# One PSUM bank for four state space transposes, and one adaLN section read in half rows in a later stage

## The chip, the cores and the metric

The kernel runs on one core of a Trainium2 chip. The metric is the device time of one execution in microseconds (us), lower is better. The core has five engines with instruction streams of their own: TensorE (PE, matmuls and transposes into PSUM), VectorE (DVE), ScalarE (ACT), GpSimd (POOL) and SyncE (SP, which here issues nearly all DMAs). Each takes its own instructions in order; between engines only semaphores order them.

## The reference, cut to what matters

One decoder layer in float32, sequence 2048, width 1024. Half of the mixing width is attention with forget gates (8 heads of 64), the other half a complex diagonal state space model (32 groups of 16 channels, 64 states each). A conditioning vector `c` makes six vectors of width 1024 (adaLN): shift, scale and gate for the mixer, and the same for the FFN.

```python
silu_c = jax.nn.silu(c)
mod = (silu_c @ w_ada[l] + b_ada[l])[:, None, :]
sh_m, sc_m, gt_m, sh_f, sc_f, gt_f = jnp.split(mod, N_MOD, axis=-1)

h = rmsnorm(x, g_mix[l]) * (1.0 + sc_m) + sh_m
q, k, v, f_logit, u = jnp.split(h @ w_in[l], [...], axis=-1)
attn = rmsnorm(forgetting_attention(q, k, v, log_f), g_attn_out[l])
ssm = rmsnorm(s5_ssm(u, ...), g_ssm_out[l])
x = x + gt_m * (jnp.concatenate([attn, ssm], axis=-1) @ w_out[l])

h = rmsnorm(x, g_ffn[l]) * (1.0 + sc_f) + sh_f
gate_pre, val = jnp.split(h @ w_up[l], 2, axis=-1)
y = (jax.nn.silu(causal_dwconv(gate_pre, ...)) * val) @ w_down[l]
x = x + gt_f * y
```

In the state space part the output is gated: `z = gelu(y)`, then `z * sigmoid(z @ w_glu + b_glu)`, per group.

## The kernel before

The sequence is cut into four blocks of 512 tokens. A float32 matmul is made of three: each operand is split into a high and a low part (`w_hi`, `w_lo`, `h_hi`, `h_lo`), and hi x hi, hi x lo and lo x hi are accumulated in PSUM. Results that a later stage needs go through DRAM scratch (`qb_d`, `kb_d`, `v_d`, `u_d`, `att_d`, `ssm_d`, `f_d`).

**What sets the order.** The program is written stage by stage. A planner then orders each engine's stream: it walks a model of the timeline, and where several instructions could go next on an engine, it takes the one that stands earliest in the program; what is written under `tc.high_priority()` goes first. The order is fixed when the kernel is built. On the chip each engine follows its stream, so an instruction whose data are late holds all that follow it on that engine. Tiles of one tag form a ring of `bufs` buffers, given out in program order: a tile waits until the last reader of the one before it in that buffer is done. When a pool is closed, the next pool takes its place in memory and waits for its last users, for single tiles where the pool was opened through `opened`.

**The input stage** (to about 350 us in the profile). The u projections of blocks 2, 3, 1 and 0 (`proj_u`), the q, k and v projections of blocks 1 and 0 (`proj_qkv`), the tables of the state space part, the forget gates' running sums, and the adaLN sections. Sections 0 and 1 are made first (`ada_first`). The other four go through `ada_late`: `ada_acc` reads the section in 8 row blocks of 128 x 1024 (512 KB, L305), in tiles of the ring `xt` with six buffers, and accumulates them with DVE (L307 the first, L309 the other seven) into `ada_acc`, a ring of two. `ada_cols` then sums over the partitions with 8 matmuls against a column of ones (L315) and adds the bias (L317), which gives the vector as 8 columns, one per 128 channels. Section 5 is `tf`, the FFN's gate; section 2 is `tm`, the mixer's gate. Both are loaded behind the forget gates, `tf` first, and their columns are made by the hook of `proj_qkv(0, ...)` behind its sixth q/k unit, when `tf` and `tm` both are pending. Then `in_ctx.close()` frees the pools of this stage, which hold the x tiles, the adaLN tiles and most PSUM banks.

**The state space stage** (to about 620 us). `ssm` goes over 16 pairs of channel groups; `stage_a` of pair p + 1 is written ahead of `stage_b` of pair p. It runs at high priority. `stage_a` loads the pair's tables (`tab`, `ft`, `ttg`, `glt`), transposes the inputs, makes the state inputs (L834) and runs the scan on DVE. `stage_b` makes the outputs (`y_ps`, L860 to L862), GELU on ACT and DVE (`z`, L869, a ring of two), the gate matmuls (`g_ps`, L874), tanh on ACT (`th`, L877), the product on DVE (L880, which writes over `th`), and the transposes back to tokens (`tr_ps`, L885), copied out by ACT (`vout`, L886). `g_ps` and `tr_ps` share the tag `out`, a ring of one PSUM bank. After every fourth pair `vout` goes to `ssm_d`.

Beside it, in program order: attention of block 0 (`attention((0,))`), then the q, k and v projections of blocks 2 and 3, which read their normalised inputs back from `f_d`. Each `proj_qkv` has 8 units for q and k (`qk`, L460) and 8 for v (L427). Their PSUM banks are `vq` and `qs`; attention's scores use the tag `sc`, a ring of two banks (`max_ps`, `am_ps`).

**Attention of one head.** `att_max` loads q into `qa` and each key block into one of the `ka` tiles, finds the row maxima (L938, L943), transposes them into a row `rrow` (L949, L951), and SP copies that into `qa` (L952). `att_main` makes the scores (L981, L982), the exponentials (L991 to L993) and the sums over values (L1002, L1006). Finished pairs of heads go to `att_d` (L1039). There are five `ka` tiles in the attention pool; a sixth, `kx`, joins for blocks 1 to 3.

**After it.** `mix_t(0)` reads attention and state space outputs back (L1178, L1179), norms the state space half (squares L1181, scale L1187), transposes it (L1191, into the ring `ff` of three banks that takes the place of projection and state space banks), splits it, and norms the attention half (L1198). Then come `out_proj(0)` (L1217), attention of blocks 1 to 3, and the FFN. `tf` is read where the down projection is added to the residual (L1279, L1419).

Of the kernel before, what the change touches and what calls it, by code (L numbers as in the profile page):

```python
# [12 lines left out]
F32 = mybir.dt.float32  # L13
F32R = mybir.dt.float32r
# [27 lines left out]
RT = 1  # L42
ATB = 1
HOOK = 5
LEAD = 4
NSC = 2

# [63 lines left out]
def hybrid_layer(ctx, tc, x, c_t, w_ada, b_col, gains, w_flat, bf_row, a_re, a_im, log_dt,  # L111
# [336 lines left out]
                Q.dma_start(u_d[t0 : t0 + P, (cc - 2) * 256 : (cc - 1) * 256], ust)  # L448
        return h

    def proj_qkv(b, h, vq_ps, hook=None):
        def qk(ms):
            ws = [weights.get(*qk_slots[m]) for m in ms]
            pss = [vq_ps() for _ in ms]
            for k in range(KT):
                hi, lo = h[k]
                for (wh, wl), ps in zip(ws, pss):
                    a, bb = wh[:, k * P : (k + 1) * P], wl[:, k * P : (k + 1) * P]
                    for i, (lt, rt) in enumerate(((a, hi), (a, lo), (bb, hi))):
                        mark[0] = T.matmul(ps, lhsT=lt, rhs=rt, start=(k == 0 and i == 0), stop=(k == KT - 1 and i == 2))  # L460
            for m, ps in zip(ms, pss):
                hi = vq_a("qk_hi", [P, TB], F32R)
                lo = vq_b("qk_lo", [P, TB], F32R)
                sc = 0.125 if m < 4 else 1.0
                A.activation(hi, ps, AF.Copy, scale=sc)
                V.scalar_tensor_tensor(out=lo, in0=ps, scalar=sc, in1=hi.bitcast(F32), op0=ALU.mult,
                                       op1=ALU.subtract)
                dst = qb_d[b] if m < 4 else kb_d[b]
                for g in range(2):
                    hd, rs = (m % 4) * 2 + g, slice(g * 64, (g + 1) * 64)  # L470
                    Q.dma_start(dst[hd, int(m < 4)], hi[rs].bitcast(F32))
                    Q.dma_start(dst[hd, int(m >= 4)], lo[rs].bitcast(F32))

        for ms in ((0,), (1,), (2,), (3,), (4,), (5,), (6,), (7,)):
            qk(ms)
            if ms == (HOOK,) and hook is not None:
                hook()
        for cc in range(2):
            sl = [weights.get(*vfu_slots[cc * 2 + kh][:2]) for kh in range(2)]
            for s in range(4):  # L480
                ps = vq_ps()
                token_rows([ps], h, s, sl, 256)
                pv = ps[:, 0:256].rearrange("p (h d) -> p h d", d=64)
# [3 lines left out]
                Q.dma_start(v_d[b][s, :, cc * 4 : cc * 4 + 4], vst.bitcast(F32))  # L487
# [310 lines left out]
    def ssm(sp, sps):  # L798
# [56 lines left out]
        def stage_b(p, vout, ft, ttg, glt, ug, hs):  # L855

            yp = sps.tile([P, 512], F32, name="y_ps", tag="y", bufs=1)
            for g in range(2):
                yo = yp[:, g * 256 : (g + 1) * 256]
                T.matmul(yo, lhsT=ttg[:, g, :], rhs=ug[:, g, :], start=True, stop=False)  # L860
                T.matmul(yo, lhsT=ft[:, 0, g], rhs=hs[:, 0, 0:256], start=False, stop=False)
                T.matmul(yo, lhsT=ft[:, 1, g], rhs=hs[:, 1, 0:256], start=False, stop=True)  # L862

            y2 = sp.tile([P, 512], F32, name="y2", tag="y2", bufs=1)
            A.activation(y2, yp, AF.Square, scale=math.sqrt(0.044715))
            V.scalar_tensor_tensor(out=y2, in0=y2, scalar=1.0, in1=yp, op0=ALU.add, op1=ALU.mult)
            A.activation(y2, y2, AF.Tanh, scale=math.sqrt(2.0 / math.pi))
            z = sp.tile([P, 512], F32, name="z", tag="z")
            V.scalar_tensor_tensor(out=z, in0=y2, scalar=1.0, in1=yp, op0=ALU.add, op1=ALU.mult)  # L869

            gp = sps.tile([P, 512], F32, name="g_ps", tag="out", bufs=1)
            th = sp.tile([P, 512], F32, name="th", tag="th")
            for g in range(2):
                T.matmul(gp[:, g * 256 : (g + 1) * 256], lhsT=glt[:, g, :], rhs=z[:, g * 256 : (g + 1) * 256],  # L874
                         start=True, stop=True)
# [4 lines left out]
            V.scalar_tensor_tensor(out=o4, in0=th, scalar=1.0, in1=z, op0=ALU.add, op1=ALU.mult)  # L880
            c0 = (p % 4) * 32
            for kb in range(2):
                pt = sps.tile([P, 512], F32, name="tr_ps", tag="out", bufs=1)
                for g in range(2):
                    T.transpose(pt[:, g * P : (g + 1) * P], o4[:, g * 256 + kb * P : g * 256 + (kb + 1) * P], ident)  # L885
                A.activation(vout[kb][:, :, c0 : c0 + 32].rearrange("k t (g c) -> k g t c", g=2),  # L886
                             pt[:, 0:256].rearrange("k (g t c) -> k g t c", g=2, t=8), AF.Copy, scale=0.25)

        vin = vout = None
        pend = None  # L890
# [185 lines left out]
    def ada_late(sec, key):  # L1076
        late_acc.append((ada_acc(sec, V), sec, key))

    def ada_cols():

        with tc.issue_after(mark[0].ins):
            while late_acc:
                acc, sec, key = late_acc.pop(0)
                ada_col(acc, prep_ps, sec, mod[key])

    ap_ = in_ctx.enter_context(tc.tile_pool(name="ada", bufs=1))
    with tc.tile_pool(name="prep", bufs=1) as pp, tc.tile_pool(name="wu", bufs=1) as wup:
        rows0 = load_x(2)
# [14 lines left out]
        forget()  # L1103
        ada_cols()
        fold_gain(mod["gf"], 8)
        ada_late(5, "tf")
        ada_late(2, "tm")
    proj_qkv(0, h, pair_ps(qs_psum), ada_cols)
    in_ctx.close()
    att_ctx = ExitStack()  # L1110
    att_pool = opened(att_ctx, "att", bufs=2, side="right")
    def aug_tiles(pool, nm, n):

        ts = [pool.tile([67, TB], F32R, name=f"{nm}{i}", bufs=1) for i in range(n)]
        for t in ts:
            G.memset(t[64:67, :].bitcast(F32), 1.0)
        return ts

    qa_t, ka_all = itertools.cycle(aug_tiles(att_pool, "qa", 2)), aug_tiles(att_pool, "ka", 5)
    ka_t = [itertools.cycle(ka_all)]  # L1120
    att_ps = opened(att_ctx, "att_ps", bufs=1, space=PSUM, side="right")
    with tc.tile_pool(name="ssm", bufs=2) as sp, tc.tile_pool(name="ssm_ps", bufs=1, space=PSUM) as sps:
        qs_ps = pair_ps(sps)
        with tc.high_priority():
            ssm(sp, sps)
        attention((0,))
        for b in (2, 3):
            h = []
            for k in range(KT):
                f = h_f()  # L1130
                Q.dma_start(f, f_d[b][k])
                h.append(split_h(f, mod["sm"][:, k : k + 1]))
            proj_qkv(b, h, qs_ps)


    cv = const.tile([P, NFF, 4], F32, name="cv")
# [9 lines left out]
    actp = opened(fp_ctx, "act", bufs=6)  # L1146
    sq_pool.append(fp)
    yt = []
    ka_t.append(itertools.cycle(ka_all + aug_tiles(fp, "kx", 1)))

    def ff_ps():
        return fps.tile([P, 512], F32, name="ff_ps", tag="ff", bufs=3)
# [538 lines left out]
```

## Time and profile before

| | us |
|---|---|
| median of 3 runs | 2689.65 |
| lowest and highest of them | 2687.12 to 2692.45 |
| the profiled execution's own time | 2689.94 |
| its span, first to last instruction | 2687.6 |
| PE busy in the span | 2576.9 (96%) |
| PE weight loads | 2081.5 (77%) |
| DVE busy | 1928.3 (72%) |
| ACT busy | 1239.2 (46%) |
| POOL busy | 190.5 (7%) |

How to read it: the profile is one execution, and its times count from the first instruction. In a timeline a row gives the start, the length, the engine, the line, the operation with output and inputs, and in brackets how long the engine had been idle and what released it. In a group of instructions (all that touch a tile, or a line) stand the count, the least, median and most ns of one, and the first and last start in us. A table of stretches gives for each its length, then busy us and instruction count of PE, PEld (weight loads), DVE, ACT and POOL, the mean granted PE clock, the busy share of the DMA engines and GB/s. A matmul's length is modelled and overlaps the next one's, so a full PE shows as busy for the whole stretch.

### The profile page before, as it was taken

What the parts mean: (1) busy time and instruction counts of PE and PEld (TensorE: products, weight loads), DVE (VectorE), ACT (ScalarE), POOL (GpSimd) and SP (SyncE); (2) the same over time, 40 slices, a digit from 0 to 9 for tenths busy, and PEclk for the clock granted to TensorE, in tenths of its full rate; (3) what the DMA queues carried; (4) which work ended last, traced back from release to release, by engine and by line L of the source; (5) the groups of instructions that cost most, each with busy time, mean ns of one, the idle gap of its engine ahead of it and who ended that gap; (6) DMA issues with size and microseconds to landing.
All of it is one profiled execution on the core that took longest, in us unless ns stands there. A gap on an engine that the chain in (4) does not pass through costs nothing. (4 is left out here: it accounts for less than half of the span.)

```text
span 2687.6 us, 35574 instructions
## 1 busy us (share of the span) xinstructions
PE 2576.9 (96%) x12343; PEld 2081.5 (77%) x12343; DVE 1928.3 (72%) x3559; ACT 1239.2 (46%) x2056; POOL 190.5 (7%) x146
## 2 busy tenths in 40 slices
PE   6999989998999999999999999999979999999997
PEld 3888768886777888888788888887858888877886
DVE  7989678876687877887976776655587777762333
ACT  3423245554365545555555555555444444442222
POOL 0001000000000000000000000000043343310000
PEclk8999989997899999999899999999989999999999
DMA  9486977665556555656465555557622323336563
GB/s 314 146 278 214 314 239 206 200 190 163 183 186 208 195 188 176 196 171 210 165 198 193 196 174 188 174 180 279 207 102 94 126 94 105 115 124 244 199 223 96
DMA packets 263043, 500.61 MB, mean 186 GB/s; under 512 B 26800, under 2 KB 111664, under 8 KB 262864
## 3 DMA queue, kind: packets, MB, share of 16 engines
q1 hardware_dynamic: 261040, 493.10, 56.0%
q0 software_dynamic: 1280, 4.20, 0.4%
q8 instruction: 97, 1.59, 0.2%
q10 hardware_dynamic: 544, 1.05, 0.1%
q14 instruction: 82, 0.67, 0.1%
HBM read 371.17 MB, written 127.01 MB: 185 GB/s over the span
## 5 line engine op out<-in xcount | busy, mean ns | idle before, releaser
L77 DVE TENSOR_TENSOR w_lo<-w_raw,w_hi 128x1024 fp32r<-128x1024 f32 (+2 forms) x219 | 236.0, 1079 | 206.3 <-ACT w_hi L76 202.2
L76 ACT CAST w_hi<-w_raw 128x1024 fp32r<-128x1024 f32 (+2 forms) x219 | 203.3, 929 | 367.8 <-PE acc_ps L1460 112.7
L1243 PE MATMUL ff_ps<-h_hi,w_lo 128*128 128x512 f32 x704 | 280.3, 398 | 0.0
L1243 PE MATMUL ff_ps<-h_hi,w_hi 128*128 128x512 f32 x704 | 280.0, 399 | 0.1
L1243 PE MATMUL ff_ps<-h_lo,w_hi 128*128 128x512 f32 x704 | 279.6, 397 | 0.0
L943 DVE TENSOR_REDUCE mx<-sc_ps 128x1 f32<-128x512 f32 (+2 forms) x320 | 195.4, 620 | 86.7 <-PE sc_ps L938 47.9
L991 ACT ACTIVATE pf<-sc_ps 128x512 f32<-128x512 f32 (+1 forms) x320 | 168.8, 542 | 186.7 <-PE sc_ps L982 87.1
L992 ACT CAST ph<-pf 128x512 fp32r<-128x512 f32 (+1 forms) x320 | 177.6, 568 | 86.5 <-PE o_ps L1002 83.4
L993 DVE TENSOR_TENSOR pl<-pf,ph 128x512 fp32r<-128x512 f32 (+1 forms) x320 | 195.1, 620 | 22.3 <-ACT ph L992 20.9
L1001 DVE TENSOR_TENSOR acc<-acc,pf 128x512 f32<-128x512 f32 (+2 forms) x264 | 159.4, 606 | 29.6 <-ACT pf L991 27.0
L1243 PEld LDWEIGHTS ff_ps<-h_hi,w_hi 128*128 128x128 f32 x704 | 133.5, 190 | 29.1 <-ACT h_hi L378 0.5
L1243 PEld LDWEIGHTS ff_ps<-h_lo,w_hi 128*128 128x128 f32 x704 | 133.5, 190 | 29.0
L1243 PEld LDWEIGHTS ff_ps<-h_hi,w_lo 128*128 128x128 f32 x704 | 133.3, 189 | 28.8
L1459 PE MATMUL acc_ps<-act,w_hi 128*128 128x512 f32 (+1 forms) x372 | 144.5, 389 | 10.6 <-DMA act<-act 6.4
L106 ACT CAST w_hi<-w_raw 128x1024 fp32r<-128x1024 f32 (+2 forms) x100 | 96.2, 962 | 123.9 <-PE ff_ps L1243 44.5
L1460 PE MATMUL acc_ps<-act,w_hi 128*128 128x512 f32 (+1 forms) x372 | 144.2, 388 | 0.0
L1461 PE MATMUL acc_ps<-act,w_lo 128*128 128x512 f32 (+1 forms) x372 | 143.7, 388 | 0.3 <-DVE w_lo L77 0.3
L1275 PE MATMUL ff_ps<-act_hi,w_hi 128*128 128x512 f32 x352 | 140.2, 399 | 0.9 <-ACT rt L366 0.9
L1276 PE MATMUL ff_ps<-act_lo,w_hi 128*128 128x512 f32 x352 | 139.4, 397 | 0.0
L1277 PE MATMUL ff_ps<-act_hi,w_lo 128*128 128x512 f32 x352 | 139.0, 396 | 0.0
L981 PE MATMUL sc_ps<-qb,kb 128*128 128x512 f32 (+2 forms) x320 | 127.9, 401 | 2.6 <-DVE mx L943 1.8
L1002 PE MATMUL o_ps<-ph,vv 128*128 128x512 f32 (+1 forms) x320 | 122.4, 383 | 1.3 <-ACT ph L992 1.3
(517 smaller groups left out, 6455.7 us busy)
## 6 DMA issues: line engine op xcount, KB each, us to landing
w_raw<-in_w_flat SPq DMA_DIRECT2D x193, 512.0 KB
w_lo<-wlo SPq DMA_DIRECT2D x68, 512.0 KB
wlo<-w_lo SPq DMA_DIRECT2D x52, 512.0 KB
w_raw<-in_w_flat SPq DMA_DIRECT2D x64, 384.0 KB
act<-act SPq DMA_DIRECT2D x44, 512.0 KB
kb<-kb SPq DMA_DIRECT2D x80, 256.0 KB
vv<-v SPq DMA_DIRECT2D x80, 256.0 KB
w_raw<-in_w_flat SPq DMA_DIRECT2D x64, 320.0 KB
```

The lines of the kernel that those rows point to most:

```text
L76: nc.scalar.copy(hi[:, :n], raw[:, :n])
L77: nc.vector.tensor_tensor(out=lo[:, :n], in0=raw[:, :n], in1=hi[:, :n].bitcast(F32), op=ALU.subtract)
L943: V.reduce_max(out=mx[:, s, ch : ch + 1], in_=ps[:, 0:n], axis=AX.X)
L991: A.activation(pf[:, cs], ps[:, cs], AF.Exp)
L992: A.copy(ph[:, cs], pf[:, cs])
L993: V.tensor_tensor(out=pl[:, cs], in0=pf[:, cs], in1=ph[:, cs].bitcast(F32), op=ALU.subtract)
L1001: eng.tensor_tensor(out=acc[j][:, cs], in0=acc[j][:, cs], in1=pf[:, cs], op=ALU.add)
L1243: T.matmul(ps, lhsT=lt, rhs=rt, start=(n == 0), stop=(n == 23))
L1275: T.matmul(ps, lhsT=a, rhs=ah[:, ts], start=(c == 0), stop=False)
L1459: T.matmul(pss[d][:, ts], lhsT=a, rhs=ah, start=st, stop=False, skip_group_check=cut)
L1460: T.matmul(pss[d][:, ts], lhsT=a, rhs=al, start=False, stop=False, skip_group_check=cut)
L1461: T.matmul(pss[d][:, ts], lhsT=bb, rhs=ah, start=False, stop=sp_, skip_group_check=cut)
```

## The change

Two edits.

1. In `stage_b`, the four transposes of a pair go into one tile of the ring `out`, all 512 columns of the bank, and the two copies by ACT follow them. Before, two transposes filled half a tile, ACT copied it, and the next two took the next tile, which is the same bank.

2. Section 5 (`tf`) leaves the input stage. A generator, `ada_mid`, makes it in two halves of 512 channels. `proj_qkv` of blocks 2 and 3 advances it by one step after each of its 8 q/k units, 16 steps in all. A step loads a half row block (128 x 512, 256 KB) and adds it with DVE; the eighth step of each half also makes 4 columns (4 matmuls and an addition) in a bank of attention's score ring. The loads use two of the five key tiles in turn (`ka3`, `ka4`), the accumulator is a ring of one in the state space pool. For that the first attention has three key tiles, and the other two are set up again (a memset each) after the projections.

```diff
-    def proj_qkv(b, h, vq_ps, hook=None):
+    def proj_qkv(b, h, vq_ps, hook=None, each=iter(())):
...
             if ms == (HOOK,) and hook is not None:
                 hook()
+            for _ in range(EACH):
+                next(each, None)
...
             c0 = (p % 4) * 32
+            pt = sps.tile([P, 512], F32, name="tr_ps", tag="out", bufs=1)
             for kb in range(2):
-                pt = sps.tile([P, 512], F32, name="tr_ps", tag="out", bufs=1)
                 for g in range(2):
-                    T.transpose(pt[:, g * P : (g + 1) * P], o4[:, g * 256 + kb * P : g * 256 + (kb + 1) * P], ident)
+                    T.transpose(pt[:, (2 * kb + g) * P : (2 * kb + g + 1) * P],
+                                o4[:, g * 256 + kb * P : g * 256 + (kb + 1) * P], ident)
+            for kb in range(2):
                 A.activation(vout[kb][:, :, c0 : c0 + 32].rearrange("k t (g c) -> k g t c", g=2),
-                             pt[:, 0:256].rearrange("k (g t c) -> k g t c", g=2, t=8), AF.Copy, scale=0.25)
+                             pt[:, kb * 256 : (kb + 1) * 256].rearrange("k (g t c) -> k g t c", g=2, t=8), AF.Copy, scale=0.25)
...
+    def ada_mid(pool, sec, key):
+
+        for hf in range(2):
+            acc = pool.tile([P, TB], F32, name="ada_mid", tag="ada_mid", bufs=1)
+            for k in range(KT):
+                wt = att_pool.tile([P, TB], F32, name="wada", tag=f"ka{3 + k % 2}", bufs=1)
+                Q.dma_start(wt, w_ada[sec, k, :, hf * TB : (hf + 1) * TB])
+                sc = sil[:, k : k + 1]
+                if k == 0:
+                    V.tensor_scalar(out=acc, in0=wt, scalar1=sc, scalar2=None, op0=ALU.mult)
+                else:
+                    V.scalar_tensor_tensor(out=acc, in0=wt, scalar=sc, in1=acc, op0=ALU.mult, op1=ALU.add)
+                if k == KT - 1:
+                    ada_col(acc, max_ps, sec, mod[key][:, hf * 4 : hf * 4 + 4], hf * 4, 4)
+                yield
...
         fold_gain(mod["gf"], 8)
-        ada_late(5, "tf")
         ada_late(2, "tm")
...
-    qa_t, ka_all = itertools.cycle(aug_tiles(att_pool, "qa", 2)), aug_tiles(att_pool, "ka", 5)
+    qa_t, ka_all = itertools.cycle(aug_tiles(att_pool, "qa", 2)), aug_tiles(att_pool, "ka", 3)
...
         attention((0,))
+        mid = itertools.chain(*(ada_mid(sp, sec, key) for sec, key in ((5, 'tf'),)))
         for b in (2, 3):
...
-            proj_qkv(b, h, qs_ps)
+            proj_qkv(b, h, qs_ps, each=mid)
...
-    ka_t.append(itertools.cycle(ka_all + aug_tiles(fp, "kx", 1)))
+    ka_t.append(itertools.cycle(ka_all + aug_tiles(att_pool, "ka", 2, 3) + aug_tiles(fp, "kx", 1)))
```

More of the change, by code (lines that the diff above doesn't have):

```diff
@@ L44 @@
 HOOK = 5
+EACH = 1
 LEAD = 4
@@ L1111, in hybrid_layer, with aug_tiles @@
     att_pool = opened(att_ctx, "att", bufs=2, side="right")
-    def aug_tiles(pool, nm, n):
-        ts = [pool.tile([67, TB], F32R, name=f"{nm}{i}", bufs=1) for i in range(n)]
+    def aug_tiles(pool, nm, n, i0=0):
+        ts = [pool.tile([67, TB], F32R, name=f"{nm}{i}", tag=f"{nm}{i}", bufs=1) for i in range(i0, i0 + n)]
         for t in ts:
```

## The prediction

> **What bounds the kernel now.** I read the page first: its span and the slices. Each digit is a fortieth of the span, 67 us.
>
> ```profile
> span 2687.6 us, 35574 instructions
> ...
> PE   6999989998999999999999999999979999999997
> ...
> PEclk8999989997899999999899999999989999999999
> ```
>
> TensorE is the bound almost everywhere, so a change pays only where PE is idle or at a lowered clock. The change touches slices 4 to 9, where two digits fall: slice 5 (PE 8) and slice 9 (PE 8, clock 7). The second view is the table of stretches; the columns used here are the length, PE busy and, after POOL's, the granted clock and the DMA share.
>
> ```profile
> 286.00:325.00 39.00, 38.89 (x243) 34.56 (x241) 29.60 (x40) 8.19 (x12) 1.00 (x2) 1.00 0.97 328
> 325.00:350.00 25.00, 14.90 (x96) 13.32 (x97) 7.49 (x17) 6.00 (x14) 0.00 (x0) 0.80 0.98 288
> 350.00:380.00 30.00, 27.91 (x144) 22.03 (x143) 27.65 (x51) 17.90 (x33) 0.00 (x0) 0.94 0.74 227
> 380.00:620.00 240.00, 238.50 (x1413) 196.65 (x1413) 191.59 (x374) 126.26 (x261) 0.52 (x1) 1.00 0.69 202
> 620.00:670.00 50.00, 38.13 (x135) 25.11 (x134) 38.24 (x96) 24.68 (x53) 0.00 (x0) 0.68 0.49 156
> ```
>
> I call length minus busy times clock the lost PE time: 25 - 14.90 x 0.80 = 13.1 us in 325 to 350, 30 - 27.91 x 0.94 = 3.8 us, 1.5 us in the long middle, and 50 - 38.13 x 0.68 = 24.1 us in 620 to 670. PE's work is the same after the change, so these 42.5 us are all that it can win here. Before 325 nothing is lost, though DMA is at 0.97.
>
> **The front, 325 to 350.** Timelines of PE, SP, DVE and POOL:
>
> ```profile
> 343.05 0.79 PE L982 MATMUL sc_ps<-qa,ka 67*128 67x512 f32 x1 [8.13 <-DMA qa<-rrow]
> ```
> ```profile
> 325.04 1.52 SPq L899 DMA_DIRECT2D vin<-u_d  x2
> ...
> 336.05 1.76 SPq L487 DMA_DIRECT2D v<-vst  x2
> 337.91 0.72 SPq L952 DMA_DIRECT2D qa<-rrow  x1
> ```
> ```profile
> L317 DVE TENSOR_TENSOR mod_tf<-prep_ps,bcol x1: 161/161/161, 306.3 to 306.3; 128x8 f32<-128x8 f32 x1
> L317 DVE TENSOR_TENSOR mod_tm<-prep_ps,bcol x1: 167/167/167, 323.9 to 323.9; 128x8 f32<-128x8 f32 x1
> ```
> ```profile
> 330.45 0.27 DVE L951 CAST rrow<-sc_ps 4x128 fp32r<-4x128 f32 x1
> ```
> ```profile
> 323.87 1.00 POOL L802 MEMSET ft<- 128x512 f32 x2 [41.40 <-PE prep_ps L315]
> ```
>
> The small row `rrow` is ready at 330.7, but SP sends it at 337.91: from 325.04 to 336.05 SP issues the first loads of the state space stage, which are ahead of it in its queue. It lands at about 343, and PE stands for 8.13 us with the rest of block 0's value projections behind it; the next matmul takes 0.79 us, twice the usual. The burst starts at 325 because the buffers of the input stage are freed then: the memset of `ft` had waited for the last column matmul of `ada_cols`, whose sum `mod_tm` follows at 323.9. The gate column `tf` was done at 306.3; `tm` comes behind it.
>
> The change takes `tf` out of this stage and leaves it `tm` alone, which then stands where `tf` stood: the buffers come free near 306 instead of 324, 18 us earlier, and the burst lies 18 us ahead of `rrow`. Eight loads of 512 KB and their DVE work go too. But the stretch 286 to 325 loses no PE time, so nothing is won in it; and the burst now meets the key stores and the value weights there, which could stall PE instead. Bounds: 0 to 13.1 us won. I take **6 us**, near the middle, since the 8.13 us have a named cause that moves, and the place that it moves to is just as full of DMA.
>
> **The transposes.** One state group pair's transposes and their evictions (count, then least, median and most ns, then first and last start); the gate matmuls of all 16 pairs; the product that comes before the gate, for the first five pairs; and DVE's timeline.
>
> ```profile
> L885 PE MATMUL tr_ps<-ident,th x4: 271/272/279, 473.3 to 478.1; 128*128 128x128 f32 x4
> L886 ACT ACTIVATE vout<-tr_ps x2: 378/382/387, 474.4 to 478.7; 128x256 f32<-128x256 f32 x2
> ```
> ```profile
> L874 PE MATMUL g_ps<-z,glt x64: 377/379/485, 387.6 to 619.1; 128*128 128x256 f32 x64
> ```
> ```profile
> L869 DVE SCALAR_TENSOR_TENSOR z<-y,y_ps x5: 670/682/687, 379.4 to 430.2; 128x512 f32<-128x512 f32 x5
> ```
> ```profile
> 483.90 0.68 DVE L880 SCALAR_TENSOR_TENSOR th<-th,z 128x512 f32<-128x512 f32 x1
> ...
> 486.87 0.66 DVE L869 SCALAR_TENSOR_TENSOR z<-y,y_ps 128x512 f32<-128x512 f32 x1
> ```
>
> The gate matmuls, both couples of transposes and the next pair's gate matmuls share one PSUM bank, so each waits for the eviction before it. From one pair's gate to the next are (619.1 - 387.6) / 15 = 15.4 us. The second couple of transposes starts some 4.7 us after the first (478.0 less 473.3; its second one is at 478.1), 3.2 us after the first eviction has ended (474.4 + 0.38), because PE is in other work by then. This cycle paces the stage, since it also holds the `z` ahead of it: `z` has two buffers, and the one at 486.87 could be written only once the product at 483.90 had read the one before the last. With four transposes at once and then two evictions, one return to PE goes, 4.7 less the 0.4 that a couple takes: 15.4 - 4.3 = 11.1 us. What is late next is the rest of the pipeline: the first five `z`, with both buffers still empty at first, came every (430.2 - 379.4) / 4 = 12.7 us. So I take 12.7 us a pair, and the stage's end comes 15 x (15.4 - 12.7) = 40 us sooner.
>
> The first eviction now waits for the second couple too, 0.4 us; no engine gets more instructions (64 transposes, 32 evictions as before). The Trainium skill's Perfetto Trace Analysis, section Matmuls, speaks against this: independent groups should rotate through banks, so that one's evacuation overlaps the next one's matmuls. Here there is no overlap to lose, with the second couple behind the eviction as it is; by the rule the cycle would be 11.5 us, which still lies under the 12.7.
>
> **What 40 us sooner is worth.** In 380 to 620 PE is full, so an earlier end of the state space stage wins nothing there: other matmuls move back. It pays after 620. SP, ACT and PE again:
>
> ```profile
> 611.43 0.32 SPq L1039 DMA_DIRECT2D att<-at  x1
> ```
> ```profile
> 623.32 0.38 ACT L886 ACTIVATE vout<-tr_ps 128x256 f32<-128x256 f32 x1 [0.53 <-PE tr_ps L885]
> ```
> ```profile
> 620.85 0.28 PE L938 MATMUL sc_ps<-ka,qa 66*128 66x256 f32 x1
> ...
> 669.10 0.78 PE L1217 MATMUL ff_ps<-yt,w_hi 128*128 128x512 f32 x1
> ```
> ```profile
> L1191 PE MATMUL ff_ps<-ident,row x16: 272/273/422, 656.8 to 660.2; 128*128 128x128 f32 x16
> ```
>
> Projections 2 and 3 end at 620.85 and the last state space eviction comes at 623.32. Its store, reload, norm, transposes and splits take until 669.10, and only block 1's attention runs beside them, badly. With the last eviction near 583, that chain lies beside dense projections. What stays exposed: the transposes use the PSUM banks that the projections held, so 669.10 - 656.8 = 12.3 us follow the projections' end, and the attention half (stored at 611.43) needs about as long. At the stretch's loss of 24.1 / 50 that is 5.9 us, so 18 us are won; bounds 0 and 24.1. I take **16 us**, because half of the moved section falls into this place.
>
> **The half rows.** The group rows of the existing sections:
>
> ```profile
> L309 DVE SCALAR_TENSOR_TENSOR ada_acc<-wada,sil,ada_acc x28: 1259/1281/1330, 142.4 to 317.8; 128x1024 f32<-128x1024 f32 x28
> ...
> L288 DVE SCALAR_TENSOR_TENSOR ada_acc<-wada,sil,ada_acc x14: 744/749/752, 16.8 to 39.4; 128x512 f32<-128x512 f32 x14
> L307 DVE TENSOR_SCALAR ada_acc<-wada,sil x4: 734/744/754, 139.3 to 298.9; 128x1024 f32<-128x1024 f32 x4
> L286 DVE TENSOR_SCALAR ada_acc<-wada,sil x2: 476/477/478, 16.3 to 27.6; 128x512 f32<-128x512 f32 x2
> ```
> ```profile
> L1279 DVE SCALAR_TENSOR_TENSOR yt<-ff_ps,mod_tf,row x16: 735/748/753, 832.1 to 1487.3; 128x512 f32<-128x512 f32 x16
> ```
>
> Removed: 0.744 + 7 x 1.281 = 9.7 us of DVE. Added: 2 x 0.477 + 14 x 0.749 = 11.4 us, where DVE is busy 191.59 of 240 us, beside PE; counted as nothing, and 11.4 us if DVE had no room. Loads are 16 of 256 KB for 8 of 512 KB, at DMA share 0.69: eight more issues on SP, about 0.3 us each like the one at 611.43, between loads of weights. The 8 column matmuls stay; two key tiles' memsets move back on an idle POOL. The result is first read at 832.1.
>
> The added wait is in the column. Its bank comes from attention's two score banks, after all of block 0's attention in program order, so the first half's column waits until about 611. The one accumulator keeps the second half from starting until then; its loads alternate two tiles. A load under pressure took 343.05 - 337.91 = 5.1 us to its reader, so a step is at most (5.1 + 0.75) / 2 = 2.9 us and eight take 23 us: the second column comes by 635. Behind it stand block 1's second score bank, two of its key tiles, and buffers that take the accumulator's place. In PE's stream the four column matmuls stand where the planner expects the bank to be free; if attention is later than that, projection and score matmuls behind them wait too, as does DVE's stream behind the second half's first row. The Trainium skill's DMA: Bandwidth & Descriptors, section Bandwidth, speaks against the halves: it wants transfers of 1 MiB or more. By the fit in its section Anatomy of one DMA (for GpSimd's path, 2.0 us plus bytes at 436 GB/s, an estimate) a half row takes 2.6 us and the eight steps 13 us, which would take the column to 625; no row here shows a lone 256 KB load.
>
> Sum: -6 - 16 = -22 us on the profiled execution's 2689.94 us (2.3 us around the span, 0.3 above the median): **2668 us**.
>
> **Rivals.**
> - Both losses go wholly: -13.1 - 24.1 = -37, 2653 us. Needs block 0's attention to end well before the projections. For it: attention gets ACT and DVE once the states are done. Against: the 12 us behind the projections.
> - Only the front pays, -6: 2684 us. The states' pace is held by the rest of the pipeline or by PE's order, and 12.7 us was measured on few pairs.
> - The lost time only moves: the burst stalls PE ahead of 325, and attention of block 0, at 611.43 as before, sets the end. 2690 us.
> - Slower: the states keep their pace, and the second half's column blocks block 1's scores. They start at 635 instead of 620.85; for 14 us the 38.13 x 0.68 / 50 = 0.52 of PE that was used goes, 7 us, and a little clock after it: +8, 2698 us. It decides once that column ends after 621 with the output projection not yet ready.
>
> **How the numbers follow.** Forecast 0.52, full 0.08, front only 0.16, moves 0.11, slower 0.13. A measurement tells about 0.2%, 5.4 us, from no change. Faster: 0.52 + 0.08 + 0.09 of the front-only case, whose 6 us lie at that bound, 0.69; same 0.07 + 0.11 = 0.18; slower 0.13. The range of 2650 to 2693 leaves out the slower case and 0.04 below. The forecast's own range is 2655 to 2680.
>
> **What would show it.** `mod_tm` near 306 and the memset of `ft` with it; no wait of 8 us for `rrow`; four transposes back to back, gates 12 to 13 us apart, the last eviction near 583; the first output projection matmul between 620 and 640; `mod_tf` in two pieces around 611 and 635. I am wrong if the gates stay 15 us apart, if block 0's attention ends later than 611, or if the clock in the 50 us before the output projection is still under 0.8.

## The result, and the profile after

| kernel | time, us (median; least to most) | profiled span, us |
|---|---|---|
| before | 2690.39 (2687.12 to 2692.45) | 2687.6 |
| changed | 2670.65 (2669.64 to 2673.3) | 2667.8 |

The ratio is 0.9934, with a 95% interval of 0.9922 to 0.9946. The forecast was 2668 us. Timed a second time, beside the experiments, the changed kernel gave 2674.2 us against 2687.6, ratio 0.9953 (0.9941 to 0.9965). So the gain is 13 to 20 us.

The same stretches as in the prediction, for the changed kernel (length, PE, PEld, DVE, ACT and POOL busy, then the granted clock, the DMA share and GB/s):

```profile
286.00:325.00 39.00, 35.85 (x202) 31.65 (x201) 19.19 (x31) 7.68 (x13) 1.00 (x2) 0.91 1.03 318
325.00:350.00 25.00, 24.67 (x178) 21.67 (x176) 19.21 (x35) 13.59 (x26) 0.00 (x0) 1.00 0.97 309
350.00:380.00 30.00, 28.12 (x140) 21.08 (x141) 28.87 (x59) 14.76 (x29) 0.00 (x0) 1.00 0.83 241
380.00:620.00 240.00, 235.90 (x1396) 197.16 (x1395) 194.32 (x376) 124.90 (x256) 1.50 (x3) 0.98 0.70 213
620.00:670.00 50.00, 44.24 (x190) 32.99 (x189) 40.19 (x93) 27.66 (x53) 0.00 (x0) 0.84 0.56 189
```

The loss in 325 to 350 has gone from 13.1 to 25 - 24.67 x 1.00 = 0.3 us, and a new one of 39 - 35.85 x 0.91 = 6.4 us has come ahead of it. The loss in 620 to 670 has fallen from 24.1 to 50 - 44.24 x 0.84 = 12.8 us, but 380 to 620 now loses 240 - 235.90 x 0.98 = 8.8 instead of 1.5: the hole behind the projections begins sooner.

The signs that the prediction listed, from the groups of instructions (count, durations in ns, first and last start) and the timelines of POOL, ACT and SP:

```profile
L318 DVE TENSOR_TENSOR mod_tm<-prep_ps,bcol x1: 161/161/161, 304.6 to 304.6; 128x8 f32<-128x8 f32 x1
```
```profile
303.84 1.00 POOL L805 MEMSET ft<- 128x512 f32 x2 [26.24 <-DMA kb<-qk_lo]
```
```profile
L877 PE MATMUL g_ps<-z,glt x64: 377/379/381, 378.4 to 563.4; 128*128 128x256 f32 x64
```
```profile
570.36 0.66 ACT L891 ACTIVATE vout<-tr_ps 128x256 f32<-128x256 f32 x2 [0.98 <-PE tr_ps L888]
```
```profile
589.74 0.32 SPq L1044 DMA_DIRECT2D att<-at  x1
```
```profile
L318 DVE TENSOR_TENSOR mod_tf<-sc_ps,bcol x2: 155/158/162, 596.0 to 617.9; 128x4 f32<-128x4 f32 x2
```
```profile
L1238 PE MATMUL ff_ps<-yt,w_hi x64: 387/393/477, 642.5 to 690.6; 128*128 128x512 f32 x64
```

The gates are (563.4 - 378.4) / 15 = 12.3 us apart (15.4 before, 12.7 forecast). The state space stage ends at 570 instead of 623, and block 0's attention at 590 instead of 611. PE's wait of 8 us for `rrow` is gone. But the first out_proj matmul comes at 642.5, just outside the 620 to 640 that the prediction gave, and the projections' last matmul ended about 612: 30.5 us between them, where the prediction had left about 12 exposed. The 50 us ahead of out_proj:

```profile
592.50:642.50 50.00, 40.13 (x223) 32.80 (x221) 33.96 (x84) 18.62 (x38) 1.50 (x3) 0.76 0.63 209
```

A clock under 0.8 there was one of the three signs by which the prediction would be wrong, and it is 0.76, so that sign came: in the tail 50 - 40.13 x 0.76 = 19.5 us are still lost.

Two places in the timelines say where the rest went. In the front, the burst of state space loads begins on SP at 305.55, and the stores of block 0's keys are now behind it. PE stops for 3.15 us at the same time. SP, PE, ACT and DVE:

```profile
305.55 1.53 SPq L904 DMA_DIRECT2D vin<-u_d  x2
...
314.90 1.27 SPq L904 DMA_DIRECT2D vin<-u_d  x2
316.27 1.43 SPq L473 DMA_DIRECT2D kb<-qk_lo  x1
```
```profile
315.76 0.58 PE L428 MATMUL vq_ps<-w_hi,h_hi 128*128 128x256 f32 x1 [3.15 <-DVE qk_lo L467]
```
```profile
311.11 0.41 ACT L827 COPY uc<-vin 128x256 f32<-128x256 f32 x1 [7.80 <-DMA vin<-u_d]
312.49 0.40 ACT L827 COPY uc<-vin 128x256 f32<-128x256 f32 x1 [0.97 <-DMA vin<-u_d]
312.80 1.04 ACT L77 CAST w_hi<-w_raw 128x1024 fp32r<-128x1024 f32 x1
313.75 0.59 ACT L466 ACTIVATE qk_hi<-vq_ps 128x512 fp32r<-128x512 f32 x1
```
```profile
313.88 1.23 DVE L78 TENSOR_TENSOR w_lo<-w_raw,w_hi 128x1024 fp32r<-128x1024 f32 x1 [7.94 <-ACT w_hi L77]
315.02 0.68 DVE L467 SCALAR_TENSOR_TENSOR qk_lo<-vq_ps,qk_hi 128x512 fp32r<-128x512 f32 x1
```

The late key store isn't what stopped PE: PE ran on at 315.76, before that store was issued (316.27). The chain goes through ACT. Two copies (`uc`) of the state space stage stand in its stream and wait for the burst's first loads, `vin`; only behind them come the cast of a weight, the eviction `qk_hi` and then DVE's `qk_lo`, which frees PE's bank.

In the tail the rows of `mix_t(0)` are loaded at 617.71, 47 us after the state space stage's last eviction and 28 us after attention's last store. Below are DVE's first and last instruction of the section's second half, PE's column matmuls, and SP:

```profile
596.06 0.48 DVE L1100 TENSOR_SCALAR ada_mid<-wada,sil 128x512 f32<-128x512 f32 x1
...
615.17 0.75 DVE L1102 SCALAR_TENSOR_TENSOR ada_mid<-wada,sil,ada_mid 128x512 f32<-128x512 f32 x1
```
```profile
615.98 1.87 PE L316 MATMUL sc_ps<-ones,ada_mid 128*128 128x1 f32 x8 [1.62 <-DVE ada_mid L1102]
```
```profile
616.70 0.47 SPq L934 DMA_DIRECT2D ka<-kb  x1
617.26 0.40 SPq L935 DMA_DIRECT2D ka<-cum  x1
617.71 0.33 SPq L1199 DMA_DIRECT2D row<-att  x1
```

The first half's column waited for block 0's attention, as forecast; the second half began when that column had freed the accumulator (596), and the row loads stand in SP's queue behind everything of it. On the chip SP waited little for the section itself from 590 to 620 (1.2 us at its loads) and longer at the stores of v (7.2 us, for the projections' results `vst`), so the rows are late by their place in SP's order rather than by a wait for the section. That the section gave them this place is a reading; the experiments test it.

### The profile page after: what moved, and what is told of

Same layout as the page of the kernel before. It is cut to its first block, busy times and chain, and to the rows that moved or that the text cites. A ratio compares the mean times of both kernels' runs of the same rounds, so it can differ in the third digit from the quotient of the medians.

```text
span 2667.8 us, 35631 instructions
## 1 busy us (share of the span) xinstructions
PE 2571.5 (96%) x12343; PEld 2082.7 (78%) x12343; DVE 1928.8 (72%) x3568; ACT 1240.3 (46%) x2056; POOL 190.4 (7%) x146
## 5 line engine op out<-in xcount | busy, mean ns | idle before, releaser
L1264 PEld LDWEIGHTS ff_ps<-h_hi,w_hi 128*128 128x128 f32 x704 | 133.1, 189 | 28.6
```

What stands on the lines that cost most here:

```text
L1264: T.matmul(ps, lhsT=lt, rhs=rt, start=(n == 0), stop=(n == 23))
```

## The experiments

Each kernel was timed beside the kernel before on one chip. Losses are length less busy times clock, from one row for each of three stretches: the front (262 to 380), the tail (600 to 800), and a hole where block 1 meets block 2's attention (1200 to 1400). The clock has two decimals, so a loss over 200 us is good to 1 us; some expectations add finer stretches, which give up to 1.5 us less. "Rows" is the first load of `mix_t(0)`'s rows, "out" the first out_proj matmul.

| kernel | time | ratio (95%) | front | tail | hole | rows | out |
|---|---|---|---|---|---|---|---|
| before | 2687 to 2690 | 1 | 22.0 | 37.0 | 10.8 | 632.5 | 669.1 |
| changed | 2670.65 | 0.9934 (0.9922 to 0.9946) | 9.5 | 28.6 | 13.1 | 617.7 | 642.5 |
| a_again | 2674.2 | 0.9953 (0.9941 to 0.9965) | 12.7 | 28.3 | 12.9 | 617.8 | 643.1 |
| e1_tr_only | 2677.7 | 0.9964 (0.9951 to 0.9976) | 20.7 | 18.8 | 17.5 | 592.8 | 639.3 |
| e2_ada_only | 2682.4 | 0.9979 (0.9970 to 0.9988) | 14.6 | 37.4 | 10.8 | 628.2 | 664.4 |
| e5_no_section | 2672.0 | 0.9940 (0.9927 to 0.9953) | 13.2 | 18.4 | 16.8 | 581.3 | 627.1 |
| e6_before_no_section | 2676.3 | 0.9960 (0.9948 to 0.9973) | 15.6 | 28.2 | 12.5 | 631.4 | 658.2 |
| e4_col_bank | 2664.8 | 0.9913 (0.9899 to 0.9927) | 13.6 | 13.1 | 14.7 | 587.9 | 629.4 |
| e3_two_acc | 2669.2 | 0.9930 (0.9918 to 0.9941) | 10.4 | 25.6 | 14.4 | 618.2 | 643.2 |
| e7_hold_rows | 2670.6 | 0.9937 (0.9924 to 0.9951) | 14.8 | 19.9 | 17.0 | 581.4 | 630.1 |
| e9_late_release | 2694.0 | 1.0010 (0.9997 to 1.0023) | 15.1 | 30.2 | 17.3 | 620.5 | 641.7 |
| e8_each2 | 2672.8 | 0.9935 (0.9914 to 0.9957) | 16.7 | 20.1 | 16.5 | 583.2 | 633.4 |
| e11_loads_only | 2693.6 | 1.0022 (1.0010 to 1.0033) | 28.0 | 29.7 | 18.4 | 625.7 | 647.5 |
| e12_mults_only | 2688.9 | 1.0002 (0.9990 to 1.0014) | 22.7 | 32.0 | 12.6 | 634.4 | 671.3 |

How a row of the table comes about, from the three stretches of before and of the changed kernel:

```profile
262.00:380.00 118.00, 103.26 (x598) 88.31 (x597) 80.59 (x152) 37.51 (x67) 5.03 (x10) 0.93 0.90 286
600.00:800.00 200.00, 185.22 (x854) 145.34 (x853) 145.35 (x280) 96.69 (x171) 0.00 (x0) 0.88 0.54 180
1200.00:1400.00 200.00, 195.00 (x883) 154.44 (x882) 164.84 (x308) 115.39 (x195) 0.00 (x0) 0.97 0.57 189
```
```profile
262.00:380.00 118.00, 111.82 (x652) 94.44 (x652) 86.04 (x176) 41.76 (x78) 4.46 (x8) 0.97 0.94 291
600.00:800.00 200.00, 188.39 (x853) 148.43 (x852) 156.76 (x303) 99.21 (x171) 1.50 (x3) 0.91 0.56 185
1200.00:1400.00 200.00, 194.69 (x868) 154.05 (x867) 159.91 (x301) 108.91 (x183) 0.00 (x0) 0.96 0.58 192
```

118 - 103.26 x 0.93 = 22.0 us lost in the front before, and 118 - 111.82 x 0.97 = 9.5 after. The two profiles of the changed kernel differ by 3.2 us in the front and 0.3 in the tail: so a difference of some 3 us in a single cell tells nothing.

### Each part by itself

The transposes alone: before, with only the edit in `stage_b`.

> Only the transposes are changed; the section stays in the input stage. Theory A (in the changed kernel the tail is held by the moved section: the first loads of out_proj's rows go out at 617.7 us, right behind the second half's column, although the state space ended at 570 and block 0's attention at 590): here nothing of the section stands in the tail, the pace of a pair falls to 12 to 13 us as there, the front keeps its loss of about 17 us (270 to 350), and the first out_proj matmul follows the projections' end by 15 to 22 us instead of 30.5: time 2671 to 2676, a gain of 14 to 19. Theory B (what holds the row loads is something else behind the projections' end, such as SP's stores of v and of the split weights, and a sooner end of the state space is worth little): the distance stays at about 30 us and the gain is 3 to 7, time 2683 to 2687.

```profile
L874 PE MATMUL g_ps<-z,glt x64: 377/379/462, 387.4 to 579.1; 128*128 128x256 f32 x64
```
```profile
262.00:380.00 118.00, 104.59 (x605) 89.77 (x605) 81.14 (x157) 37.98 (x68) 5.44 (x10) 0.93 0.90 287
600.00:800.00 200.00, 190.70 (x918) 153.25 (x917) 152.17 (x297) 102.91 (x173) 0.00 (x0) 0.95 0.58 192
1200.00:1400.00 200.00, 194.10 (x855) 152.36 (x854) 156.46 (x297) 107.70 (x179) 0.00 (x0) 0.94 0.54 176
```

The pace is (579.1 - 387.4) / 15 = 12.8 us. The front is as before, and the tail loses 18.8 instead of 37.0: 18.2 us won there, and out_proj is 14 us behind the projections' end at 625. Theory A has the tail right. The time fell by only 10.2 us, between the two theories: the hole at 1200 to 1400 has grown by 6.7.

The section alone: the changed kernel with the transposes of before.

> Only the section is moved; the transposes keep their two turns of a bank. Both theories: the front gains 10 to 13 us as the stretches of the changed kernel say (mod_tm near 305, loss between 270 and 350 down from about 17 to about 7). Theory A: block 0's attention ends near 600 to 610, the second half is multiplied after it, its column comes near 625 to 640, and the row loads behind it are no sooner than the 632.5 of before: the tail gains nothing or loses up to 6; time 2676 to 2686. Theory B: the section in the tail costs nothing; time 2675 to 2679.

5.5 us faster, in theory A's range and above B's. The front wins 7.4 us, not 10 to 13, and the tail nothing (37.4); the gates stay 15.5 us apart (first 382.9, last 614.9), and the rows are loaded at 628.2, behind the state space stage's last eviction (621.2). The two parts by themselves give 10.2 + 5.5 = 15.7 us, between the 13 and the 20 of the whole change.

No section at all, with the old and with the new transposes:

```diff
-        mid = itertools.chain(*(ada_mid(sp, sec, key) for sec, key in ((5, 'tf'),)))
+        V.tensor_copy(mod['tf'], bcol[:, 40:48])
...
-            proj_qkv(b, h, qs_ps, each=mid)
+            proj_qkv(b, h, qs_ps)
```

> Kernel before with the section left out altogether (its eight columns are the bias alone), transposes as before. It measures the front by itself: if the stretches of the changed kernel are read rightly, 10 to 13 us less than before (2675 to 2680); if the front is worth only the 6 us of the prediction, 2682 to 2686, and the remaining gain of the changed kernel comes from the tail after all.

> Changed kernel with the section of the FFN's gate left out altogether (its eight columns are the bias alone). Theory A: without the second half the row loads go out near the end of the projections (600 to 612), and the first out_proj matmul comes 15 to 20 us behind them instead of 30.5: 2655 to 2662, 9 to 16 less than with the section. Theory B: the row loads stay near 616 and the time is within 4 us of the changed kernel, 2667 to 2672.

With the old transposes the time falls by 11.6 us, 6 more than when the section is only moved. That is in the range expected for a front worth 10 to 13 us, but not for that reason: the front wins 6.4 us and the tail 8.8. The tail's 28.2 against 37.4 can't be put down to the section's late place, though: the kernel before, which makes the section in the front, loses 37.0 there. So with the old transposes a cost of that place is not shown. With the new transposes the rows are loaded at 581.3, out_proj begins at 627.1, and the tail loses 18.4 instead of 28.3 to 28.6. Theory A holds for the tail, but the time (2672.0) is that of the changed kernel: theory B's number. Most of the ten microseconds won in the tail are lost again in the hole at 1200 to 1400 (+3.7), in the front (0.5 to 3.7 more than in the two profiles of the changed kernel) and in 1800 to 2000 (26.0 against 23.6). So theory A was right about the place and wrong about the sum.

### What holds the row loads

Two edits for the two waits of the section, the bank of its columns and its one accumulator:

```diff
-                    ada_col(acc, max_ps, sec, mod[key][:, hf * 4 : hf * 4 + 4], hf * 4, 4)
+                    ada_col(acc, qs_ps, sec, mod[key][:, hf * 4 : hf * 4 + 4], hf * 4, 4)
```

> Changed kernel, but the section's columns are made in the projections' pair of banks, so that the first one need not wait for block 0's attention (594 us there) and the one accumulator comes free near 353. Both theories: first column near 355 to 370, second near 400 to 420, row loads at 575 to 590 as in the kernel without the section (581), loss of TensorE time between 600 and 700 us about 17 (changed kernel 22, without the section 17). Theory C (what is won before 800 is given back, because out_proj that starts sooner meets less of the next blocks' attention done, and the holes at 1200 to 1400 and 1800 to 1900 grow by 5 to 7, as in the two kernels with early row loads so far, 17.5 and 16.6 us against 11.6 and 13.0): time 2667 to 2673, no better than the changed kernel. Theory D (those holes differ by the order that the planner happens to give): 2660 to 2665.

The columns came at 451 and 589 instead of 355 to 370 and 400 to 420: they no longer follow the end of block 0's attention (its last store is at 596.0); that their places in PE's stream set them is likely, but not tested. The rows were loaded at 587.87, and the tail's loss fell below that of the kernel without the section:

```profile
600.00:800.00 200.00, 194.73 (x940) 156.53 (x940) 152.91 (x290) 99.12 (x162) 0.00 (x0) 0.96 0.56 188
```

200 - 194.73 x 0.96 = 13.1 us, 15 less than the changed kernel. The time, 2664.8, is under theory C's range and at the upper end of D's; the hole is 14.7, not 16 to 17. Timed side by side with the changed kernel it is faster (0.9913 against 0.9953, intervals apart), and it has the lowest time of all versions: about 23 us under the kernel before.

```diff
-            acc = pool.tile([P, TB], F32, name="ada_mid", tag="ada_mid", bufs=1)
+            own, tag = (pool, "ada_mid") if hf else (att_pool, "ka4")
+            acc = own.tile([P, TB], F32, name="ada_mid", tag=tag, bufs=1)
...
-                wt = att_pool.tile([P, TB], F32, name="wada", tag=f"ka{3 + k % 2}", bufs=1)
+                wt = att_pool.tile([P, TB], F32, name="wada", tag="ka3", bufs=1)
```

> Changed kernel, but the first half is summed in a tile of its own (the buffer of the second load; loads go through one buffer then), so that the second half is read and multiplied by about 420 and only its column waits. If the one accumulator is what keeps the second half back, both columns come right behind block 0's attention (594 to 597 instead of 596 and 618) and the row loads near 598 to 606 instead of 617.7; the loss between 600 and 650 falls from 19.5 to 8 to 14. Theory C: time 2666 to 2672; theory D: 2660 to 2666.

```profile
L318 DVE TENSOR_TENSOR mod_tf<-sc_ps,bcol x2: 154/154/155, 616.2 to 617.5; 128x4 f32<-128x4 f32 x2
```

The columns are 1.3 us apart instead of 21.9: the second half is multiplied by 426 now, so the accumulator was what had held it. But they did not come near 595. Block 0's attention, whose last store was at 589.7, now ends at 610.8, and the first column follows it, which is the score bank's wait. With the single load buffer attention ends 21 us later, which was not foreseen; the rows came at 618.2, and the ratio (0.9930) is close to the changed kernel's first one (0.9934).

> The kernel without the section (eight columns are the bias alone), with one tile more in the state space's pool that is written behind the last matmul of the projections: the rows of out_proj, which take that space, are held to about 616 us instead of 581, as the section holds them to 617.7, and nothing else is added. Theory C: the loss between 600 and 700 rises from 17 to 20 to 25, the hole at 1200 to 1400 falls from 16.6 to 11 to 14, and the time stays within 4 us of 2672. Theory D: the holes behind 1200 stay as they were and the time is 2675 to 2682.

```diff
+        hold = sp.tile([P, TB], F32, name="hold", tag="hold", bufs=1)
+        with tc.issue_after(mark[0].ins):
+            V.memset(hold, 0.0)
```

The tile was written at 305.7, and the first row went out at 581.4 as without it. So the edit held nothing, and the run tells neither theory; it repeats the kernel without the section (tail 19.9 and 18.4, time 2670.6 and 2672.0). The next edit, on the kernel with the columns in the projections' banks, puts true data in the way:

```diff
+        late = sp.tile([P, TB], F32, name="ada_mid", tag="ada_mid", bufs=1)
+        V.memset(late, 0.0)
+        pl_ps, seen = qs_ps(), small.tile([P, 1], F32, name="seen", tag="seen", bufs=1)
+        T.matmul(pl_ps[:, 0:1], lhsT=late[:, 0:P], rhs=ones[:, 0:1], start=True, stop=True)
+        V.tensor_copy(seen, pl_ps[:, 0:1])
```

> The kernel with the columns in the projections' banks (2664.8 us, row loads from 588, loss of TensorE time 12.7 us between 600 and 800 and 75.5 up to 800), with one thing added: behind the last matmul of the projections the accumulator's buffer is written with zeros and read once more by one matmul, so that the rows of out_proj, which take its place, are loaded no sooner than about 621, as the section holds them in the changed kernel (617.7, 10 us behind the projections' end). If the late row loads are what the moved section costs in the tail: loss between 600 and 800 up to 20 to 28 us, first out_proj matmul at 640 to 650 instead of 629, 2669 to 2676 us. If the gain of that kernel came from something else (its front or the order of the later blocks): loss between 600 and 800 at 12 to 16 and 2662 to 2668.

The tail's row, and the row loads in SP's timeline:

```profile
600.00:800.00 200.00, 186.57 (x869) 149.85 (x870) 145.36 (x281) 95.53 (x163) 0.00 (x0) 0.91 0.56 185
```
```profile
619.49 0.94 SPq L490 DMA_DIRECT2D v<-vst  x2
620.49 0.44 SPq L1204 DMA_DIRECT2D row<-att  x1
```

One zeroing, one matmul and one copy make the kernel 27 us slower than the one they were added to, by the spans. The rows go out 33 us later, out_proj 12 us later, and the tail loses 200 - 186.57 x 0.91 = 30.2 us instead of 13.1: 17 of those 27 us (2690.1 and 2663.1). The time is 18 us above the expected range, and the rest of the 27 us lies elsewhere, so this edit moved more than the rows. The added matmul itself ran at 622.5, after the first row load: the chip did not make the rows wait for that tile. They stood in SP's order behind the last stores of v, and that order is made when the kernel is built.

The tails of all kernels with the new transposes fall into two groups. Where the rows are loaded by 593 (e1, e4, e5, e7, e8), 13.1 to 20.1 us are lost; where they come at 617 to 621 (the changed kernel twice, e3, e9), 25.6 to 30.2. So late row loads go with the cost of the moved section in the tail, some 6 to 10 us; that they alone make it is not shown, since each edit also changes the rest of the built order.

Nor does the hole at 1200 to 1400 go with the row loads: it is 17.3 us in e9 with late rows, and 16.8 without the section with early ones, so theory C, that a gain in the tail is given back there because of it, falls. What sets the hole is open.

> The kernel with the columns in the projections' banks, and two steps of the section for each of the projections' parts instead of one (EACH = 2), so that the whole section lies in block 2's projections: both columns before about 460 us instead of 451 and 589, and the row loads behind nothing but the state space's own buffers (575 to 590). Its row loads are then no longer the section's affair: if 588 was still late for them, the loss between 600 and 800 falls by 1 to 4 us, 2660 to 2665; if not, the time is that of the other kernel within 3 us, unless the sixteen loads and multiplies, twice as dense, hold up block 0's attention on VectorE in the front (then mod_tm stays near 305 but the first output of attention comes later than 400, and the loss between 286 and 380 grows from 12.5 to 15 or more).

The columns came at 403 and 454 and the rows at 583, 5 us sooner, but nothing was won: the time is 8 us longer, with ratios whose intervals overlap, and the loss is 3.1 us more in the front and 7.0 in the tail. So the date of the row loads isn't all that made the other kernel fast; what else differs between the two orders is not settled. Attention's first output came at about 403 against 400, so VectorE was hardly held up.

### What the section cost in the front

```diff
-        ada_late(5, "tf")
+        for k in range(KT):
+            wt = xp.tile([P, D], F32, name="wada", tag="xt", bufs=XB)
+            Q.dma_start(wt, w_ada[5, k])
+            V.tensor_scalar(out=mod["tf"][:, k : k + 1], in0=wt[:, 0:1], scalar1=sil[:, k : k + 1], scalar2=None, op0=ALU.mult)
```

> Kernel before, with the section's eight loads kept in the input stage, and in place of its eight multiplies of 128x1024 and its columns eight of 128x1 (the section is left out but for its transfers). Without the section at all the loss of TensorE time between 262 and 380 fell from 20.9 to 15.9 us and the time by 11.6. If the front was held by the transfers (the share of the DMA engines there is 0.92 to 0.98), it stays as before: loss 19 to 22, 2684 to 2690 us, although mod_tm comes earlier than 323.9. If it was held by VectorE and by the buffers that wait for it, as the prediction has it, the front is that of the kernel without the section: mod_tm at 306 to 312, loss 14 to 17, 2675 to 2681.

```diff
-            wt = xp.tile([P, D], F32, name="wada", tag="xt", bufs=XB)
-            Q.dma_start(wt, w_ada[sec, k])
+            if sec != 5 or k == 0:
+                wt = xp.tile([P, D], F32, name="wada", tag="xt", bufs=XB)
+                Q.dma_start(wt, w_ada[sec, k])
```

> Kernel before, with the section's eight multiplies and its columns kept in the input stage, but only one of its eight loads (all eight multiply the same tile: the sums leave out seven eighths of the section's rows). If the transfers held the front: mod_tm at 306 to 314, loss between 262 and 380 14 to 17, 2675 to 2681 us. If VectorE held it: mod_tm at 316 to 324 and 2683 to 2690.

Each half of the section alone keeps the front's loss, 28.0 and 22.7 us against 22.0, so neither theory is enough. With the multiplies alone `mod_tm` comes at 317.5, the burst after it at 321, and the time is 2688.9: all as VectorE's theory had it. The loads alone were slower (2693.6 us) and lost more (28.0) than either theory expected. With the loads alone `mod_tm` is at 307.7 and the burst begins at 312.0, as VectorE's theory wanted. Yet PE waits longer than before, for a weight whose load is behind the burst and the key stores that follow it. SP, then PE's timeline:

```profile
312.01 1.34 SPq L899 DMA_DIRECT2D vin<-u_d  x2
...
321.37 1.27 SPq L899 DMA_DIRECT2D vin<-u_d  x2
...
328.13 1.09 SPq L68 DMA_DIRECT2D w_raw<-in_w_flat  x2
```
```profile
333.23 0.58 PE L427 MATMUL qs_ps<-w_hi,h_hi 128*128 128x256 f32 x1 [13.02 <-ACT w_hi L76]
```

In these three kernels the burst holds SP for about 10 us, and PE stands for something that hangs on it: `rrow` before (8.13 us) and a value weight here (13.02), both behind it in SP's queue, and in the changed kernel the work behind ACT's wait for `vin` (3.15). SP itself waited little in the burst (0.5 us from 325 to 338 before, 0.7 us from 312 to 323 here): its many issues took the time. At the stores of v it is otherwise: in e9 SP waited there 9.9 us between 600 and 624 for DVE's `vst`, and the row loads went out behind them. The Trainium skill's DMA: Bandwidth & Descriptors, section Anatomy of one DMA, says that a DMA's wait for a semaphore is made by the sequencer that issues it, before dispatch; the stores of v in e9 agree with that.

How much the front gives varies with the built order. In the ten profiles without the section there (the two of the changed kernel, e2 to e9), 9.5 to 16.7 us are lost from 262 to 380; with the whole section there 22.0 (before) and 20.7 (e1). The changed kernel's first profile is the lowest of the ten.

> The changed kernel itself, timed beside the three others: 2668 to 2673, ratio 0.992 to 0.995.

2674.2 us and 0.9953 lie just above both ranges: two timings of one kernel differ here by up to 0.2%.

## Why the prediction was right

The time, 2670.65 us, is 2.65 above the forecast, and both parts paid, as the forecast had it. But its terms were not all of the right size, the sign of the clock ahead of out_proj (0.76) spoke against it, and that the sum came so close is in part luck.

- **Transposes, -16 us.** Right, for the transposes by themselves. The pace by itself is 12.8 us (12.7 forecast), so the shared bank's cycle did set it before; what sets the 12.8 was not tested. The tail's gain alone is 18.2 us, of which the time kept 10.2, as the hole at 1200 to 1400 grew. The caution of the Trainium skill's Perfetto Trace Analysis, section Matmuls, is that independent groups should rotate through banks. The trace does not bear it out here: with four transposes in one bank the stage is faster, 12.8 us a pair against 15.4.
- **Half rows, counted as nothing.** This is the step that failed. With the new transposes they cost 6 to 10 us in the tail (25.6 to 28.6 us lost with them late, 18.4 to 19.9 without them there). The prediction saw the wait, its order and its duration: 19.9 us for the eight steps (596.06 to 615.17 and 0.75), under its bound of 23. The 13 us, an estimate from the fit in the Trainium skill's DMA: Bandwidth & Descriptors, section Anatomy of one DMA, are too short beside these 19.9. The prediction named "buffers that take the accumulator's place" behind the wait, and did not price what follows them: out_proj's rows, whose last store had gone out at 589.7 and which were loaded at 617.7.
- **Front, -6 us.** Near the truth for the section by itself, too small for this kernel: 7.4 us with the section moved alone, 6.4 with it left out, and 12.5 in the changed kernel (9.3 in its second profile). The named cause, the burst ahead of `rrow`, moved as described, and the burst did stall PE elsewhere, for 3.15 us, though through ACT and not at the key stores. But the stretches from 262 to 286 and from 350 to 380 won too (3.1 and 1.9 us), and the experiments show loads and multiplies each enough to keep the loss, which the prediction's one cause does not explain. Why the front gains as much as it does stays open.
- **Sum.** -12.5 in the front, -1.5 in the long middle, -8.4 in the tail and +2.3 in the hole at 1200 to 1400 make -20.1. The other stretches add 2.2, so the whole is -17.9; the spans differ by 19.8, which is as near as a clock of two decimals comes. The sum was right because the front's surplus stands against the half rows' price. The prediction had neither at its size, so that they cancel is luck.
- **The rivals.** The slower case needed the second column after 621 and the states at their old pace; the column came at 617.9, and the pace fell. Its mechanism, a late second half that holds up the tail, is real all the same, but the row loads came late instead of the scores. It is not all that kept off the full gain: e4, with early rows, still lost 13.1 us in the tail and won 23 us, not 37. The front-only case fails, since the tail gained 8.4 us here and 18.2 in e1. The loss did move in part (6.4 us from 286 to 325), but not wholly.

## What to carry to other kernels

When work is moved into a stage that hides its arithmetic, look up what its last instruction holds: its buffers, its bank's ring, and the place of the next stage's first loads in the queue of the engine that issues them. Here the multiplies of the first half cost nothing that shows (0.3 us of PE time is lost from 325 to 350, where most of them ran), and a late place in SP's order went with 6 to 10 us. Look for a PSUM bank in a ring whose other users run beside the moved work (the projections' banks: 2664.8 us), not in one whose users must all end first (attention's: 2670.7 and 2674.2). Time it all the same: with two steps a part, the projections' banks gave 2672.8 us.

## What was not expected

- One tiny chain (a zeroing, a matmul on one column, a copy) behind the projections made the kernel 27 us slower, more than the whole change had won; the row loads moved behind the last stores of v in the built order.
- Losses sum up as the spans do only when later stretches are counted: the hole at 1200 to 1400, which no edit touches, varied from 10.8 to 18.4 us over these kernels.
- The half row's eight loads and multiplies took 2.5 us each with two load tiles, at a DMA share of 0.79 (596 to 616); with one load tile, block 0's attention ended 21 us later.
